# Rotation of 96 images by 180 degrees: the first load in three transfers instead of one

## The chip, the core and the metric

The kernel runs on one core of a Trainium2 chip. A core has several engines with instruction streams of their own, which meet at semaphores. Three matter here: VectorE (DVE in the profile) copies data within the on-chip memory; SyncE (SP) issues DMAs and waits for semaphores before it issues them; sixteen DMA engines move the data between HBM and the on-chip memory. The on-chip memory has 128 partitions, and a tile here is a row of float32 numbers in each of them.

The metric is the device time of one execution in microseconds (us), as the median of several runs.

## The reference

```
batch, c, h, w = 32, 3, 256, 256
x = np.random.randn(batch, c, h, w).astype(np.float32)

def reference(x):
    return np.rot90(x, k=2, axes=(-2, -1)).astype(np.float32)
```

Each of the 32 x 3 = 96 images of 256 x 256 is turned by 180 degrees. Read as a line of 65,536 numbers, an image is simply reversed. 25.17 MB are read and as many written.

## The kernel before

The 96 images are taken in three strips of 32 images. In a strip each image is cut into four quarters of `E` = 16384 numbers (64 KB), so that a strip fills 128 partitions with a row of 64 KB each, in tiles `A`, `Bt` and `Ct` for strips 0, 1 and 2. A fourth tile `T` of 2048 numbers per partition is scratch. All three strips lie on the chip at once; no tile is used twice.

The reversal is split in two. `inside` reverses each row in place on VectorE: for four pairs of blocks of 2048 numbers it copies the far block reversed into `T`, the near block reversed into the far place, and `T` into the near place (three copies a pair, all on line 52). The four quarters of an image change places in the store: the output is addressed with its quarters in reverse order (lines 58 and 59).

All DMAs are issued by SP, in the order of the code: the load of `A` (line 69), the load of `Bt`, then `Ct` in a body of 58 KB and a tail of 6 KB per row (`TAIL` = 1536 numbers), then the stores. They go through one queue, which its DMA engines empty in order. Strip `A` is stored in two pieces: the first 128 numbers of each row (`LEAD`), and the rest. The second of these also waits, by a dependency added by hand, until the body of `Ct` has landed. `Bt` and `Ct` are each stored in one piece when VectorE is done with them.

A copy on VectorE waits for the load of the numbers that it reads or overwrites, and a store for the copies that wrote its numbers. The framework places these waits: one semaphore for each DMA in flight, one for VectorE. Where an instruction has more waits than it can carry itself, the queue gets small waiting instructions ahead of it.

Of the kernel before, what the change touches and what calls it, by code (L numbers as in the profile page):

```python
# [2 lines left out]

os.environ.setdefault("NEURON_RT_ULTRASERVER_MODE", "4")

# [4 lines left out]


@with_exitstack
def kernel(
    ctx: ExitStack,
    tc: tile.TileContext,
    x: bass.AP,
    out: bass.AP,
):

    nc = tc.nc
    P = 128

    B, C, H, W = x.shape
    L = H * W
    G = 32
    E = L // 4
    J = E // 8

    x4 = x.rearrange("b c h w -> (b c) (h w)").rearrange(
        "(g n) (s e) -> g (n s) e", n=G, s=4)
    o4 = out.rearrange("b c h w -> (b c) (h w)").rearrange(
        "(g n) (s e) -> g n s e", n=G, s=4)  # L40

    pool = ctx.enter_context(tc.tile_pool(name="slots", bufs=1))
    A = pool.tile([P, E], x.dtype, tag="A")
    Bt = pool.tile([P, E], x.dtype, tag="B")
    Ct = pool.tile([P, E], x.dtype, tag="C")
    T = pool.tile([P, J], x.dtype, tag="T")

    def back(t, lo, hi):
        return t[:, hi - 1:(lo - 1 if lo else None):-1]

    def copy(dst, src):
        tc.keep_in_program_order(nc.vector.tensor_copy(out=dst, in_=src))  # L52

    def load(t, g, lo, hi):
        return nc.sync.dma_start(out=t[:, lo:hi], in_=x4[g][:, lo:hi])  # L55

    def store(t, g, lo, hi):
        return nc.sync.dma_start(
            out=o4[g][:, ::-1, lo:hi], in_=t[:, lo:hi])

    def inside(t):
        for lo in range(0, E // 2, J):
            hi = E - lo - J
            copy(T[:, :], back(t, hi, hi + J))
            copy(t[:, hi:hi + J], back(t, lo, lo + J))
            copy(t[:, lo:lo + J], T[:, :])

    TAIL = 1536
    load(A, 0, 0, E)
    load(Bt, 1, 0, E)  # L70
    body = load(Ct, 2, 0, E - TAIL)
    load(Ct, 2, E - TAIL, E)
    inside(A)
    LEAD = 128
    store(A, 0, 0, LEAD)
    first = store(A, 0, LEAD, E)
    tc.add_manual_dep(
        first.ins, body.ins.name,
        mybir.DependencyInfo(mybir.DependencyClass.Sync, mybir.DependencyReason.DATA),
        reason="the first store is queued while the last strip is on its way")  # L80
    for g, t in ((1, Bt), (2, Ct)):
        inside(t)
        store(t, g, 0, E)


# [1 line left out]
_INS = ['x']  # L87
_OUTS = [((32, 3, 256, 256), 'float32')]


# [23 lines left out]
```

## Time and profile before

| | us |
|---|---|
| median of 7 runs | 122.16 |
| lowest and highest run | 121.97, 122.73 |
| the profiled execution | 122.0 |
| its span in the profile | 120.2 |
| VectorE busy, 36 copies of 1.227 us | 44.2 |
| DMA: 50.33 MB in 1152 packets, 419 GB/s over the span | |

The profiled execution's time is 1.8 us longer than its span, which runs from the first instruction in the profile to the last. A packet is what one DMA engine moves as one piece: here one row of a transfer, or the 4-byte message to a semaphore that ends a transfer on that engine. A transfer of 128 rows gives each of the sixteen engines eight rows and one such message. The share of a DMA queue is the time that its packets took, as a part of sixteen engines' time in the stretch that is asked for. Rows of SP's queue have the start and the duration of the issuing instruction; the time to landing runs from the issue until the last message has come.

### The profile page before, as it was taken

How to read it: one execution, taken by the hardware profiler on the slowest of the kernel's cores; microseconds unless marked ns; L12 is line 12 of the kernel's file. 1: busy time of each engine (PE TensorE's matmuls, PEld its weight loads, DVE VectorE, ACT ScalarE, POOL GpSimd, SP SyncE). 2: the span in 40 equal slices, each digit the busy share in tenths (PEclk: the TensorE clock that was granted, in tenths of full speed). 3: DMA queues.
4: the chain of work that ended last, by engine and by line, in shares of the span. 5: the costliest groups of instructions: out<-in, count | busy, mean ns of one | idle time of the engine just before them, and what ended most of it. 6: DMA issues, size and time to landing. Idle time of an engine off the chain costs nothing.

```text
span 120.2 us, 95 instructions
## 1 busy us (share of the span) xinstructions
DVE 44.2 (37%) x36; POOL 0.2 (0%) x4
## 2 busy tenths in 40 slices
DVE  0000000499995099999059999400000000000000
POOL 0000000000000000000000000000000000000000
DMA  9888988899889979879499777988898889888980
GB/s 349 349 349 349 676 371 349 349 632 414 349 349 611 403 316 573 375 316 632 192 438 692 346 346 346 692 349 349 349 698 349 349 349 698 349 349 349 676 371 0
DMA packets 1152, 50.33 MB, mean 419 GB/s; under 512 B 128, under 2 KB 256, under 8 KB 384
## 3 DMA queue, kind: packets, MB, share of 16 engines
q1 hardware_dynamic: 1152, 50.33, 97.4%
HBM read 25.17 MB, written 25.17 MB: 419 GB/s over the span
## 4 chain that ended last, share of the span: by engine, by line
DMA 34%; DVE 25%; another core or an unknown queue 4%; issue 1%; SPq 0%; DVEq 0%
DMA Bt<-in_x_dram 34%; DVE T L52 8%; DVE Bt L52 8%; DVE Ct L52 8%; SPq L55 0%; DVEq L52 0%
## 5 line engine op out<-in xcount | busy, mean ns | idle before, releaser
L52 DVE COPY T<-A 128x2048 f32<-128x2048 f32 x4 | 4.9, 1227 | 22.8 <-DMA A<-in_x_dram 22.7
L52 DVE COPY T<-Ct 128x2048 f32<-128x2048 f32 x4 | 4.9, 1227 | 4.5 <-DMA Ct<-in_x_dram 4.4
L52 DVE COPY T<-Bt 128x2048 f32<-128x2048 f32 x4 | 4.9, 1227 | 4.4 <-DMA Bt<-in_x_dram 4.3
L52 DVE COPY Bt<-T 128x2048 f32<-128x2048 f32 x4 | 4.9, 1227 | 0.1
L52 DVE COPY Bt<-Bt 128x2048 f32<-128x2048 f32 x4 | 4.9, 1227 | 0.1
L52 DVE COPY A<-A 128x2048 f32<-128x2048 f32 x4 | 4.9, 1227 | 0.1
L52 DVE COPY Ct<-T 128x2048 f32<-128x2048 f32 x4 | 4.9, 1227 | 0.1
L52 DVE COPY A<-T 128x2048 f32<-128x2048 f32 x4 | 4.9, 1227 | 0.1
L52 DVE COPY Ct<-Ct 128x2048 f32<-128x2048 f32 x4 | 4.9, 1227 | 0.1
L98 POOL MEMSET const-bfloat16-1.0<- 128x1 bf16 x1 | 0.1, 101 | 0.0
L98 POOL MEMSET const-uint8-127<- 128x1 uint8 x1 | 0.1, 101 | 0.0
L98 POOL MEMSET const-float32-0.0<- 128x1 f32 x1 | 0.1, 98 | 0.2 <-issue 0.2
L98 POOL MEMSET const-float32-1.0<- 128x1 f32 x1 | 0.1, 98 | 0.0
## 6 DMA issues: line engine op xcount, KB each, us to landing
out_dram<-A SPq DMA_DIRECT2D x1, 8128.0 KB, 21.2
Ct<-in_x_dram SPq DMA_DIRECT2D x1, 7424.0 KB, 57.9
Ct<-in_x_dram SPq DMA_DIRECT2D x1, 768.0 KB, 59.3
out_dram<-A SPq DMA_DIRECT2D x1, 64.0 KB, 35.2
A<-in_x_dram SPq DMA_DIRECT2D x1, 21.9
Bt<-in_x_dram SPq DMA_DIRECT2D x1, 40.8
out_dram<-Bt SPq DMA_DIRECT2D x1, 39.8
out_dram<-Ct SPq DMA_DIRECT2D x1, 42.8
```

Of the source, the lines that this page charges most:

```text
L52: tc.keep_in_program_order(nc.vector.tensor_copy(out=dst, in_=src))
L98: nc = _bacc.Bacc("TRN2", target_bir_lowering=False, num_devices=1)
```

## The change

Line 69 is replaced by a loop of three loads into the same tile. They bring the first 512 numbers of each row (2 KB), the next 1024 (4 KB) and the remaining 14848 (58 KB). They are issued one after the other ahead of the load of `Bt`. Nothing else is edited: `inside(A)`, which begins by reading the last 2048 numbers of a row and then overwrites them with the first 2048, now has waits for three loads instead of one, and the second store of `A` has waits for all of them.

```
     TAIL = 1536
-    load(A, 0, 0, E)
+    for lo, hi in ((0, 512), (512, 1536), (1536, E)):
+        load(A, 0, lo, hi)
     load(Bt, 1, 0, E)
     body = load(Ct, 2, 0, E - TAIL)
     load(Ct, 2, E - TAIL, E)
```

On SP, `load` stands before as one instruction for 128 x 16384 numbers and after as three, for 128 x 512, 128 x 1024 and 128 x 14848. The order of the instructions on VectorE is the same, and no other queue has DMAs.

More of the change, by code (lines that the diff above doesn't have):

```diff
@@ L68 @@
     TAIL = 1536
-    load(A, 0, 0, E)
+    for lo, hi in ((0, 512), (512, 1536), (1536, E)):
+        load(A, 0, lo, hi)
     load(Bt, 1, 0, E)
```

## The prediction

> **What bounds the kernel now.** I read the page first, for the engine that has no idle time.
>
> ```profile
> span 120.2 us, 95 instructions
> DVE 44.2 (37%) x36; POOL 0.2 (0%) x4
> ...
> DMA packets 1152, 50.33 MB, mean 419 GB/s; under 512 B 128, under 2 KB 256, under 8 KB 384
> ## 3 DMA queue, kind: packets, MB, share of 16 engines
> q1 hardware_dynamic: 1152, 50.33, 97.4%
> ```
>
> VectorE is busy for 37% of the span; the sixteen DMA engines for 97.4% of it. All eight DMAs go through one queue: 8 x 128 rows of data and 8 x 16 tiny completion packets make the 1152. To see where the other 2.6% lie, I asked for the DMA packets of the stretch from 1.7 to 119.1 us alone:
>
> ```profile
> q1 hardware_dynamic: 1152, 50.33, 99.8%
> ```
>
> So from the first packet to the last the engines hardly pause, and the idle time is the 1.7 us before and the 1.1 us after. A change here can act in three ways only: more packet time, a different start, or a new pause. Next, the waits of VectorE and of SP's queue:
>
> ```profile
> DVE T L52 <- DMA A<-in_x_dram: 22.7, 1, 22.7
> DVE T L52 <- DMA Ct<-in_x_dram: 4.4, 1, 4.4
> DVE T L52 <- DMA Bt<-in_x_dram: 4.3, 1, 4.3
> ...
> SPq L58 <- DMA Ct<-in_x_dram: 33.1, 2, 32.5
> ```
>
> VectorE always waits for loads, never a load for VectorE: it has 4.3 us to spare after strip A and 4.4 us after B. The SP line is the wait of the second store of A for the body of C (32.5 us), which sets when the store is queued.
>
> Now the price of a packet. The share of the queue, times 16 engines, times the length of the stretch, over the packets, is the mean time of one packet. The stretches are, in order, 5.5 to 19 us (64 KB rows of A), 42.6 to 55.5 (58 KB rows of C), 59.2 to 60.5 (6 KB rows of C's tail) and 118 to 120.2 (completions alone):
>
> ```profile
> q1 hardware_dynamic: 80, 5.24, 89.6%
> ...
> q1 hardware_dynamic: 96, 5.70, 102.0%
> ...
> q1 hardware_dynamic: 86, 0.53, 98.6%
> ...
> q1 hardware_dynamic: 16, 0.00, 0.4%
> ```
>
> They give 0.896 x 16 x 13.5 / 80 = 2.419 us, 1.020 x 16 x 12.9 / 96 = 2.193 us, 0.986 x 16 x 1.3 / 86 = 0.238 us, and 0.004 x 16 x 2.2 / 16 = 9 ns. (A packet counts whole where it begins, so a stretch can pass 100%.)
>
> Last, the start: SP's issues, and the packets that begin in 0 to 4 us, then in 1.75 to 2, 2 to 2.3 and 2.3 to 3 us.
>
> ```profile
> 0.73 0.38 SPq L55 DMA_DIRECT2D A<-in_x_dram  x1
> 1.16 0.43 SPq L55 DMA_DIRECT2D Bt<-in_x_dram  x1
> 1.63 1.01 SPq L55 DMA_DIRECT2D Ct<-in_x_dram  x2
> ```
> ```profile
> q1 hardware_dynamic: 16, 1.05, 77.4%
> ...
> q1 hardware_dynamic: 11, 0.72, 893.8%
> ...
> q1 hardware_dynamic: 3, 0.20, 176.4%
> ...
> q1 hardware_dynamic: 2, 0.13, 47.3%
> ```
>
> The first packets begin at 1.76 us, which is 0.65 us after SP has finished its first issue (0.73 + 0.38 = 1.11), and the last of the sixteen engines begins at 2.69 us in the packet records. The first packet of an engine takes 0.774 x 16 x 4.0 / 16 = 3.10 us on the mean, where later ones of the same size take 2.42: a start-up excess of 0.68 us. In the records it runs from 0.20 us (the engine that began last) to 1.09 us.
>
> **The change, part by part.**
>
> Packets. Each engine has 8 rows of a load. Two more DMAs are 16 more data packets and 2 more completions per engine; the bytes stay. What a packet costs beyond its bytes: 64 KB and 58 KB rows differ by 6144 bytes and 2.419 - 2.193 = 0.226 us, and a 6 KB packet takes 0.238, so 12 ns by the views; the packet records, whose medians are 2418, 2192 and 234 ns, give 8 ns. I take 8, since the stretch at 59.2 us holds a few packets that waited for the store behind them, and keep 12. That is 16 x 8 + 2 x 9 = 0.146 us, with 12 ns 0.21 us. It lies on the path, since the engines have no idle time that could cover it: **+0.15 us**.
>
> SP's issues. Two more of 0.43 to 0.48 us each put B's issue from 1.16 to some 2.1 us and C's tail from 2.1 to 3.0 us. Their packets are not due before A is read (20 us), so this is hidden for B and C. For A itself it is not free: the second transfer's issue ends near 1.59 us, its packets can begin 0.65 us later, at 2.24, and the third's at about 2.7. The first transfer occupies an engine for 8 rows of 2 KB at (0.226 / 3 + 0.008) = 83 ns, 0.67 us, plus at least the 0.20 us of excess: from 1.76 to 2.63 at the earliest. 2.24 comes before that. If the engines get their descriptors in turn over 0.93 us (1.76 to 2.69) and one DMA's turn begins after the last one's, the last engine begins its first transfer at 2.69, has done it at 3.56, and gets the second at 3.62: a pause of 0.06 us. The second lasts 8 x 0.158 = 1.27 us, past the third's arrival. I take 0 and keep 0.06.
>
> The start-up excess. No row shows a 2 KB packet as the first one. The bounds are that the whole mean excess goes (-0.68 us), and that it comes back once at each of the two new hand-overs (+1.36). I take 0: the first request goes out 0.65 us after the same first issue, the first issue is the same instruction, and the hand-overs that the trace has, from A to B and from B to C, show no excess (2418 to 2422 ns per packet on both sides of the first in the records).
>
> Waits. VectorE's first copy of A waits for the third transfer, which carries elements 14336 to 16383; the second, which reads the first 2048, waits for the other two, long landed. A few waits of under 0.1 us, within its 4.3 us. On SP the first store of A waits for the first transfer and that copy, as before; the second, queued behind the body of C, waits for two transfers more. SP's last satisfied wait stood 47 ns before the issue (59.528 to 59.575 us in the trace's SP rows), so two waits behind the body's could put the issue 0.09 us later. Behind that store on SP stand the stores of B and C, neither due yet (B's is issued at 60.2 and its packets start after 80 us). The cover of the second store is C's tail and the 512-byte store, 8 x 0.234 + 8 x 0.027 = 2.1 us (packet records). It is just used up: when each packet is joined to the one whose end it follows, four engines show pauses of 19 to 82 ns near 60.75 us, the only ones in the trace, and they end 0.25 us before the last engine. So a further 0.09 us on them does not reach the end; if it reached the last engine too, +0.09.
>
> Sum: 0.146 + 0 + 0 + 0 = +0.15 us. The profiled execution took 122.0 us, of which 120.2 is span and 1.8 lies around it: 120.2 + 0.15 + 1.8 = 122.15. The median of the runs is 0.16 above the profiled one, so **122.31 us**, +0.1%, where 0.3% (0.37 us) is about what a measurement of this kernel can tell from no change.
>
> The hand-overs that the trace has cost nothing that can be seen: 99.8% from first packet to last, over seven of them. What remains open is whether 0.67 us of work is enough to have the next DMA queued. A rule speaks against the change: the Trainium skill, "DMA: Bandwidth & Descriptors", section "Rules for kernel authors", asks for 1 MiB or more in each DMA (the first two transfers here are 0.26 and 0.52 MB), and the section "Anatomy of one DMA" gives a lone DMA issued from GpSimd a fixed cost of about 2.0 us. By that, two more DMAs would be an estimated +4.0 us, 126.2.
>
> **The rivals.**
>
> Faster: the start-up excess depends on the length of the first packets. For it: it is 0.68 us per engine, the only idle DMA time before the end that isn't SP's issue, and it is not one constant latency, since the engine that began last paid 0.20 and others up to 1.09. Against it: nothing ties it to length. All of it gone gives 122.31 - 0.68 = 121.63. It decides from 0.52 us on (0.37 + 0.15).
>
> Slower: the 2 KB transfer does not bridge to the second, so the engines pause, or the excess is paid again at a hand-over. For it: the margin is only 0.4 us for the first engine and -0.06 for the last. Against it: the full hand-overs elsewhere, with descriptors long queued. Paid once it gives 122.31 + 0.68 = 122.99, at both hand-overs 123.67. It decides from 0.22 us on (0.37 - 0.15).
>
> No effect even of the packets: were their 8 ns overlapped at the start, 122.16. That is the same class as my forecast.
>
> **How the numbers follow.** Same within 0.3%: 0.50, as the priced terms, 0.15 to 0.21 + 0.06 + 0.09 = 0.36, stay inside it; its own range is 122.1 to 122.5. Faster 0.24, slower 0.26: two unknowns of about equal size on both sides, the known cost leaning to slower. For eight in ten the range runs from the faster rival in full, 121.6, to nearly one repeated excess, 122.9.
>
> **What would show it.** 1440 packets, 160 under 512 B and 672 under 8 KB. The wait for A's load near 22.8 us instead of 22.65, B's and C's landings later by the same 0.15. The share from first packet to last still 99.8%. The forecast is wrong if the wait for A's load ends before 22.3 or after 23.1, which would put the difference in the first 5 us, or if the landings agree and the second store of A starts late.

## The result and the profile after

The changed kernel takes 123.31 us as the median of 13 runs (122.04 to 124.02), the kernel before 122.13 us in 34 runs beside them. The ratio is 1.0082, with a 95% interval of 1.0063 to 1.0101: **slower by 0.8%**, some 1.0 us. (The ratio leaves out runs over 1.5% above the kernel's fastest one, which are its three slowest; the plain medians are 1.2 us apart.) The forecast was 122.31 and no change that can be told, with a range of 121.6 to 122.9. It was wrong.

The profiled execution of the changed kernel took 123.59 us, with a span of 121.8 against 120.2. From its page, the span and the DMA lines:

```profile
span 121.8 us, 99 instructions
...
DMA packets 1440, 50.33 MB, mean 413 GB/s; under 512 B 160, under 2 KB 288, under 8 KB 672
## 3 DMA queue, kind: packets, MB, share of 16 engines
q1 hardware_dynamic: 1440, 50.33, 96.4%
```

The packet counts are the ones forecast. VectorE's waits (total, times, longest, in us):

```profile
DVE T L52 <- DMA A<-in_x_dram: 23.9, 1, 23.9
DVE T L52 <- DMA Ct<-in_x_dram: 4.6, 1, 4.6
DVE T L52 <- DMA Bt<-in_x_dram: 4.3, 1, 4.3
```

The load of A ends 1.2 us later than before, not 0.15; the two other waits are nearly as before. So most of the loss exists at 24 us and is carried along. Where it comes from is seen in the DMA view of three stretches of the changed kernel: from the first packet to the last (1.7 to 120.7 us), 4.55 to 6.2 us, and 61.4 to 62.2 us.

```profile
q1 hardware_dynamic: 1440, 50.33, 98.7%
...
DMA packets 1, 0.06 MB, mean 36 GB/s; under 512 B 0, under 2 KB 0, under 8 KB 0
...
DMA packets 4, 0.02 MB, mean 31 GB/s; under 512 B 0, under 2 KB 0, under 8 KB 4
```

The first line says that there is now idle time between the first packet and the last (99.8% before). The second is its source. Fifteen engines go from their 4 KB rows to the long ones without a pause and begin their first 58 KB row between 4.07 and 4.51 us, as the packet records show; **one, done with its 4 KB rows at 4.29 us like the others, begins at 4.94 us, 0.65 us later, and needs 3.23 us for it instead of 2.19**. At 8.17 us it has done its first row when the others ended theirs at 6.26 to 6.70. The late one stays late, since each engine moves its own eight rows of every transfer. The landing records of the third transfer have fifteen messages between 22.36 and 22.75 us, and the sixteenth at 23.84; for the body of C it is 59.25 to 59.65, and 61.02.

The third line shows what the others do meanwhile. The second store of A is issued when the body of C has landed on all engines, at 61.11 us instead of 59.58, and its first packet begins at 62.31 us, 1.2 us after the start of the issue. In the 0.8 us of the view only four packets begin, all four 6 KB rows, which the late engine alone still has. Joined packet by packet, the other fifteen pause for 1.0 to 1.5 us there. The late engine has no such pause, and the last landing of all moves from 119.40 to 120.94 us.

The sum for the profiled executions: +1.21 us at the last landing of A's load (22.63 to 23.84), of which 0.15 is packets; +1.51 at the body of C, where the late engine's last row took 2.56 us instead of 2.19 while the others worked on small packets; +1.54 at the last landing. The late engine's landing of A is 1.28 us behind the mean of the other fifteen: nearly all of that is two terms of equal size: it begins its long rows 0.64 us after their mean start, and has 0.67 us more of the start-up excess in them (1.03 us, all in the first row, against 0.36).

### The profile page after: what moved, and what is told of

It is laid out like the page before. It is cut to its first block, busy times and chain, and to the rows that moved or that the text cites. A ratio compares the mean times of both kernels' runs of the same rounds, so it can differ in the third digit from the quotient of the medians.

```text
span 121.8 us, 99 instructions
## 1 busy us (share of the span) xinstructions
DVE 44.2 (36%) x36; POOL 0.2 (0%) x4
## 2 busy tenths in 40 slices
DMA packets 1440, 50.33 MB, mean 413 GB/s; under 512 B 160, under 2 KB 288, under 8 KB 672
## 3 DMA queue, kind: packets, MB, share of 16 engines
q1 hardware_dynamic: 1440, 50.33, 96.4%
## 4 chain that ended last, share of the span: by engine, by line
DMA 34%; DVE 24%; another core or an unknown queue 4%; SPq 1%; issue 1%; DVEq 0%
DMA Bt<-in_x_dram 34%; DVE T L52 8%; DVE Ct L52 8%; DVE Bt L52 8%; SPq L55 1%; DVEq L52 0%
## 5 line engine op out<-in xcount | busy, mean ns | idle before, releaser
L52 DVE COPY T<-A 128x2048 f32<-128x2048 f32 x4 | 4.9, 1226 | 24.0 <-DMA A<-in_x_dram 23.9
```

## The experiments

Each is compared with the kernel before on the same chip: e1 to e4 ran on one, e5 to e8 on a second, e9 to e12 on a third, e13 to e15 on a fourth. Edits are shown against the changed kernel (against the kernel before for e7, e8 and e11 to e13); where only lines with + are shown for the load of A, they stand in place of its loop or line. A hand-over is an engine's step from the rows of one transfer to those of the next. "Late" means that an engine begins its first long row of A clearly after the others, having stood still at the hand-over. The theories, named by letters, are set out in the expectations.

**e1: without the 4 KB transfer.**

```
-    for lo, hi in ((0, 512), (512, 1536), (1536, E)):
+    for lo, hi in ((0, 512), (512, E)):
```

> The changed kernel without the 4 KB transfer: 2 KB, then 62 KB of each row. Theory A (lagging engine): where the short first transfers hand over to long rows, one of the sixteen DMA engines begins late, and it is never overtaken, so its delay is the kernel's. One short hand-over, with only 0.67 us of work ahead of it, is enough: the last landing of the load of A is 0.5 us or more behind the second last, and the time is +0.4 to +1.2 us over the kernel before (122.5 to 123.4). Theory B (number of transfers): each extra transfer costs the same 0.5 us, so half of the change's +1.0, near 122.65, with landings spread evenly. Theory C (barrier): the loss is the pause of the other engines in front of the second store of A; it follows the lag, as in A.

122.09 us, ratio 0.9995 (0.9982 to 1.0008): no change. All long rows begin between 2.66 and 3.11 us. From 3.2 to 5 us, before the first of them can have ended, no packet begins:

```profile
DMA packets 0, 0.00 MB, mean 0 GB/s; under 512 B 0, under 2 KB 0, under 8 KB 0
```

So a 2 KB transfer ahead, with 0.67 us of work in it, bridges to the next one. That refutes theory A in the form stated, and theory B, by which each transfer costs the same.

**e2: the same 6 KB ahead, in one transfer.**

```
+    for lo, hi in ((0, 1536), (1536, E)):
```

> 6 KB, then 58 KB of each row: the same bytes ahead of the long rows as in the change, in one transfer instead of two. Theory A, if the late engine comes from a queue that ran dry: the first transfer lasts 8 x 0.234 = 1.9 us and the next is issued 0.43 us after it, so no lag, and +0.08 us for 8 packets and a message (122.2). Theory A, if the late engine comes from short packets as such (engines that start nearly together and then hinder each other in the long rows): lag and +0.4 to +1.2 us remain. Theory B: +0.5.

122.04 us, ratio 0.9992 (0.9982 to 1.0001). The long rows begin at 4.15 to 4.55 us, at the same time as the fifteen of the change, and none is late: from 4.6 to 6.2 us, where the change has its late start, no packet begins.

```profile
DMA packets 0, 0.00 MB, mean 0 GB/s; under 512 B 0, under 2 KB 0, under 8 KB 0
```

With the same bytes in front, two transfers instead of three remove the loss.

**e3: three transfers, all long.**

```
+    for lo, hi in ((0, 4096), (4096, 8192), (8192, E)):
```

> Three transfers as in the change, but of 16, 16 and 32 KB of each row. Theory A: the first packets are long, the start-up excess is paid inside them as before (mean first packet 0.68 us above the later ones of its size), no engine lags: +0.15 us, 122.3. Theory B (number of transfers): +1.0, as the change.

122.06 us, ratio 0.9998 (0.9983 to 1.0012). Three transfers as such cost nothing that can be told.

**e4: the change without the gate of the second store.**

```
-    first = store(A, 0, LEAD, E)
-    tc.add_manual_dep(first.ins, body.ins.name, ...)
+    store(A, 0, LEAD, E)
```

> The changed kernel without the dependency of the second store of A on the body of C, so that this store is queued at about 41 us and no engine has to pause for it. Theory A: the lagging engine has no pause of its own, so the other engines' 1.0 to 1.5 us of pause vanish from the packet records and the time stays at +1.0 (123.1), the others being done early. Theory C (barrier): the time falls back to that of the kernel before, 122.1 to 122.4.

124.34 us, ratio 1.0179 (1.0154 to 1.0204): slower still. The pause at the second store is gone from the packet records, and the time did not fall to 122.4 as theory C wanted it, that the pause is the loss. In this profile four engines are late, beginning at 5.07, 5.40, 5.47 and 5.99 us, after pauses of 0.8 to 1.9 us at the hand-over from the second to the third transfer. The stretch from 4.45 to 6.2 us of this kernel:

```profile
DMA packets 4, 0.24 MB, mean 136 GB/s; under 512 B 0, under 2 KB 0, under 8 KB 0
```

**e8: the kernel before without that gate**, the control for e4, by the same edit.

> The kernel before without the dependency of the second store of A on the body of C; the control of the changed kernel without it. If what that one lost beyond the changed kernel (1.0 us more) belongs to the missing dependency, this one is 0.5 to 1.0 us slower than the kernel before; if it was only a larger lag at the start of those executions, this one takes 122.1 to 122.4, as the lag of its engines is small.

123.11 us, ratio 1.0062 (1.0033 to 1.0091). The gate is itself worth some 0.8 us, which accounts for most of the 1.0 us that e4 lost beyond the change. With it, theory C would have given e4 122.4 + 0.8 = 123.2 us; it took 124.3, so the pause of the fifteen is not the loss. Without the gate the change costs 124.34 - 123.11 = 1.2 us (on two chips), about what it costs with it. The page's row for the tail of C in this kernel (KB, us to landing) has 60.5 where the kernel before has 59.3:

```profile
Ct<-in_x_dram SPq DMA_DIRECT2D x1, 768.0 KB, 60.5
```

After four runs the question was why only the change's series has late engines. New theories said what delivers a transfer to an engine, and when.

**e5: four transfers, three of them tiny**, so that every engine runs dry at each hand-over.

```
+    for lo, hi in ((0, 128), (128, 256), (256, 384), (384, E)):
```

> The first load as four transfers, of 0.5, 0.5, 0.5 and 62.5 KB of each row. The short ones last only 8 x 0.027 = 0.2 us on an engine, so every engine runs dry at each hand-over and the first packet of each transfer shows when that transfer reached the engine. Theory D1 (one transfer after the other): spreading a transfer over the engines takes a fixed 0.9 us or more, so the first packets of the four come at about 1.8, 2.7, 3.6 and 4.5 us or later, with a spread over the engines. Theory D2 (two at a time): the third comes only after the first has landed, the fourth after the second. Theory D3 (delivery is slow only beside full data traffic): the four come 0.47 us apart as they are issued, at 1.8, 2.2, 2.7 and 3.2 us. Time: by D1 and D2 +1 to +2.5 us, by D3 +0.5 to +0.9.

123.49 us, ratio 1.0097 (1.0059 to 1.0136). The first rows of the last transfer begin from 3.18 us on, as theory D3 has it, and one after the other 0.9 us each (D1) is refuted: the fourth is there where D1 wanted it at 4.5 or later. With so little traffic the long rows begin on time, the first 0.65 us after the end of SP's issue (2.53 us); D2 is not told apart here. The time is above D3's bound, and the reason is in the stretch from 3.16 to 3.85 us, and in VectorE's wait:

```profile
q1 hardware_dynamic: 43, 1.03, 457.6%
```
```profile
DVE T L52 <- DMA A<-in_x_dram: 23.6, 1, 23.6
```

4.576 x 16 x 0.69 is 50.5 us; 27 of the 43 packets are small ones of some 27 ns, and the sixteen long ones take (50.5 - 0.7) / 16 = 3.11 us each, where the later ones take 2.36. The start-up excess, 0.75 us on the mean, is paid in full by the first long rows, although the engines had been at work since 1.75 us. With long rows that begin at 3.18 to 3.80 us instead of 1.76 to 2.69, that makes up the loss without a late engine.

**e6: the short transfer second, after a long one.**

```
+    for lo, hi in ((0, 4096), (4096, 4608), (4608, E)):
```

> The first load as 16, 2 and 46 KB of each row, so that the short transfer comes after 5 us of other work. Theory D1: the third transfer has been delivered by 6 us and is due at about 8 us: no pause, no lagging engine, +0.15 us. Theory D2: the third is delivered only after the first has landed at about 7.9 us, and the 2 KB transfer covers 0.67 us of the delivery: a pause of 0.5 us or more on all engines, +0.6 us or more.

121.99 us, ratio 0.9985 (0.9970 to 0.9999). The third transfer's rows begin at 7.80 to 8.25 us, on each engine right after its last 2 KB row, and on three engines before the first one's last message comes at 7.96. The pause of 0.5 us or more on all engines, by which D2 was to be known, is not there; D2 is refuted.

**e7: the change's split, but on the load of B.**

```
-    load(Bt, 1, 0, E)
+    for lo, hi in ((0, 512), (512, 1536), (1536, E)):
+        load(Bt, 1, lo, hi)
```

(A comes in one transfer.)

> A comes in one transfer again; the load of B is split into 2, 4 and 58 KB of each row instead, which is the same number of transfers, packets and messages, but their turn comes at 22 us, when all have long been issued. If the loss of the change comes from the hand-overs of the first 5 us: no pause, no lagging engine, +0.15 us (122.3). If short transfers ahead of long ones cost this wherever they stand: +1.0.

122.09 us, ratio 0.9988 (0.9973 to 1.0002). The same packets and messages at 22 us cost at most what was priced. The loss belongs to the first microseconds. (The change itself was not run on the chip of e5 to e8, so that e6 and e7 have no late engine beside them there; e1 and e2 have one on theirs with e4, and e14 with e13 and e15.)

**e9: the changed kernel again.**

> The changed kernel once more, for a second profile. Theory D3 (the descriptors of the third transfer reach some engines late because the first two already move data at full rate): again one or more engines begin their 58 KB rows 0.4 us or more after the others, though not the same delay, since the runs of this kernel lie between 122.04 and 124.02; the last landing of A's load minus 22.63 us (the kernel before) gives the lag of the span within 0.4 us. If no engine is late and the span is over 121 us, the theory falls.

123.8 us, ratio 1.0134 (1.0116 to 1.0151). Four engines are late this time, at 5.15, 5.17, 5.85 and 6.13 us, twelve begin between 4.17 and 4.59. The stretch from 4.62 to 6.2 us, and VectorE's wait:

```profile
DMA packets 4, 0.24 MB, mean 150 GB/s; under 512 B 0, under 2 KB 0, under 8 KB 0
```
```profile
DVE T L52 <- DMA A<-in_x_dram: 24.5, 1, 24.5
```

The last landing of A's load is at 24.43 us, 1.80 later than before; the span is 122.0, 1.8 longer. Which engines are late, and by how much, differs from execution to execution. The ratio here, of three runs, lies above the first one's interval (1.0063 to 1.0101), so the price of the change is no fixed number: some 1.0 us there and 1.6 here.

**e10: each short transfer twice as long.**

```
+    for lo, hi in ((0, 1024), (1024, 3072), (3072, E)):
```

> 4, 8 and 52 KB: as many transfers and as many descriptors ahead of the long rows as in the change, each short one twice as long, so the long rows are due at about 1.76 + 0.4 + 8 x (0.159 + 0.31) = 5.9 us instead of 4.1 to 4.5. Theory D3 (late delivery, up to 4.9 us in the change's profile and 6.0 in that without the gate): most of the loss is gone, 0 to +0.4 us. Theory E (the engine stumbles after a given number of descriptors, 18, or at the second message, whenever that is): +1.0 us as the change.

122.4 us, ratio 1.0024 (1.0011 to 1.0037), so 0.3 us where the change itself lost 1.6 on the same chip (e9). The long rows begin at 6.11 to 6.86 us, none late, after as many packets and messages as in the change. Theory E is refuted. The 0.3 us that remain agree with the packets' 0.15 and a little more start-up excess (0.86 us per engine on the mean of the packet records, against 0.68 before), paid mostly by the 4 KB packets here (up to 1.41 us for one).

**e11 and e12: delivery measured by itself.** Five loads of 0.5 KB per row from ScalarE's queue, beside 16 KB rows from SP, and alone.

```
+    for n in range(5):
+        nc.scalar.dma_start(out=T[:, n * 128:(n + 1) * 128], in_=x4[1][:, n * 128:(n + 1) * 128])
```

(The edit is e11's, which also loads A in 16 and 48 KB per row; e12 has the five in A and ahead of SP's first load, which overwrites them, with SP's loads kept in the order of the code. One run each.)

> A comes as 16 and 48 KB from SP, and beside it ScalarE's queue issues five loads of 0.5 KB per row into the scratch tile (work that the change does not have), so that the time tells little; the start of the 512-byte packets tells when each of the five was delivered while 16 KB packets of 0.61 us keep the engines busy until about 7 us. Issued 0.47 us apart from 0.73 us, they are due at 1.8, 2.2, 2.7, 3.2 and 3.6 us. Theory D3: the later ones come 0.5 us or more beyond that plus a packet of 0.61 us, on some engines over 1 us beyond. If delivery is not slowed: all within 0.65 us of the due time.

> The same five loads of 0.5 KB per row from ScalarE's queue, but SP's first load waits for them, so that they are delivered with no other traffic (the whole kernel begins some 4 us later by that). Both theories: first packets within 0.2 us of 1.8, 2.2, 2.7, 3.2 and 3.6 us on all engines.

Alone (126.32 us in all), they came on time: the first packets of the five at 1.74, 2.28, 2.79, 3.27 and 3.71 us, the last of each at most 0.55 us after its first, where 0.2 had been expected on all engines. Beside traffic the measurement failed (and VectorE's first copy waited until 62.8 us for the five loads into `T`, so that the kernel took 140.35 us). The two queues took turns packet by packet, so a packet's start tells when its turn came, not when it was delivered: from 8 to 42 us each began 286 packets. From 0 to 8 us, with ScalarE's queue as q10:

```profile
q1 hardware_dynamic: 160, 2.88, 90.3%
q10 hardware_dynamic: 144, 0.07, 2.8%
...
T<-in_x_dram ACTq DMA_DIRECT2D x5, 64.0 KB, 41.0
```

**e13: e2 with a tiny transfer between the two**, which makes the long rows third.

```
+    load(A, 0, 0, 1536)
+    load(T, 1, 0, 128)
+    load(A, 0, 1536, E)
```

> 6 KB and 58 KB of A, as in the version of two transfers that cost nothing, but SP issues a load of 0.5 KB per row into the scratch tile between them (work that the change does not have; it lasts 0.22 us on an engine). The long rows are thus the third transfer, issued at 1.63 us, and due after 8 x 0.234 + 0.22 = 2.1 us of work, a little more than in the change, with no 2 KB packet and no split of the 6 KB. Theory D3 (position and issue time of the long rows): late engines as in the change, +0.5 to +1.5 us. Theory F (2 KB packets and their hand-over): no late engine, +0.1 to +0.3.

122.49 us, ratio 1.0038 (1.0018 to 1.0058), with runs from 122.28 to 123.47. The profiled execution is the slowest of ten runs, and in it one engine pauses for 1.28 us and begins its long rows at 5.71 us, the others at 4.29 to 4.97. From 5 to 6.5 us:

```profile
DMA packets 1, 0.06 MB, mean 40 GB/s; under 512 B 0, under 2 KB 0, under 8 KB 0
```

No 2 KB packet and no split of the 6 KB is needed for a late engine, and theory F, by which there was to be none, is refuted for this execution. The median is another matter: its 0.32 to 0.46 us (by medians and by the ratio) lies between F's range and D3's, and 0.22 us of it are the added transfer's own work. So most executions may have no late engine, or one that is hardly late. And here the long rows are third and also issued 0.46 us later than in e2; the run doesn't tell the two apart.

**e14: the change's three transfers, the last two exchanged.**

```
+    for lo, hi in ((0, 512), (1536, E), (512, 1536)):
```

> The three transfers of the change with the last two exchanged: 2, 58, 4 KB. Same packets, messages and issues; the long rows are issued second, at 1.16 us, and the third transfer is due only at 20 us. Theory D3: no late engine, as with 2 and 62 KB, 0 to +0.15 us. Theory B (number of transfers at the start, or more issues in a row on SP): +1.0.

122.06 us, ratio 0.9990 (0.9978 to 1.0003), no engine late: the long rows begin at 2.61 to 3.16 us, and from 3.2 to 5 us no packet begins, as in e1. This undoes the loss by the order alone.

**e15: four short transfers of 2 KB.**

```
+    for lo, hi in ((0, 512), (512, 1024), (1024, 1536), (1536, 2048), (2048, E)):
```

> 2, 2, 2, 2 and 56 KB of each row: four short transfers of 0.67 us each, issued 0.47 us apart, the long rows fifth, issued at 2.6 us and due after 2.7 us of work, near 5 us. Theory D3 (delivery under full traffic is late by up to 2 to 3 us on some engines): pauses of some engines already between the short transfers, from the third on, and long rows that begin late on several: +1 us or more. If only the third transfer is slow for some reason: pauses there alone, and the fifth on time.

123.73 us, ratio 1.0131 (1.0088 to 1.0175). The landings of the four spread out as they go on: 2.79 to 3.66 us, 3.72 to 4.28, 4.50 to 5.71, 5.33 to 6.94. Some engines pause already between the short transfers, from about 3.5 us on, and the long rows begin anywhere from 5.01 to 6.61 us. It isn't the third alone.

What the runs show together: the long rows begin on time when their transfer is the second (e1, e2, e14), when it is due only at 6 us or later (e3, e6, e10, and B in e7), and when there is little traffic (e5, e12). In a series of three or more with the engines at full rate and a turn that comes at 3.5 to 5 us, one or several engines go without their next rows, for 0.65 us in the change and up to 2.1 us in e9 (the others are e4, e13 and e15). **The latest engine then sets the time**: the waits for A's load of 22.5 to 22.7 us go with spans of 120.1 to 120.3 where the gate stands, 23.0 with 120.6, and 23.6 to 24.5 with 121.7 to 122.0 (e14 stands apart, since its first copy waits for the second of its three transfers alone). That delivery to an engine is what is late, and not the engine that fails to take it up, is the reading that these conditions suggest. No run separates the two, since the profile has no record of a delivery. Nor does any run tell whether what SP goes on to issue in those microseconds, the loads of B and C (until 3.51 us in the change), has a part in it. That a late engine makes the loss is shown; why it is late is open.

## Why the prediction was wrong, point by point

- **Packets, +0.15 us: right.** 1440, 160 and 672 were counted. In the change's profile the fifteen engines that were not late landed A at 22.36 to 22.75 us, the kernel before at 22.16 to 22.63.
- **SP's issues, taken as 0 with 0.06 kept: this step failed.** It let the third transfer reach every engine at about 2.7 us, 0.65 after the end of its issue, a distance read where nothing was moving yet, and so allowed for no pause behind 1.9 us of work. One engine paused for 0.65 us there and began the third only at 4.94 us (the change); in e9 it was 6.13 and in e4 5.99 on the latest. Whether the transfer came late to it or was taken up late stays open. The 0.06 was worked out for the second transfer, where nothing went wrong. The step's comparison also named the wrong hand-over as the narrow one: the 0.67 us of the 2 KB transfer suffice (e1, e14), while after the two together, 8 x 0.083 + 8 x 0.158 = 1.9 us of work, an engine stood still.
- **The start-up excess, taken as 0: nearly right in sum, wrong in place.** It does not vanish with short first packets. In the change's packet records it is 0.77 us per engine on the mean, against 0.68 before: 0.27 in the 2 KB rows, 0.09 in the 4 KB rows, and 0.40 in the long rows, of which the second to fourth take up to 2.50 us instead of 2.19. But the late engine has 1.03 us of it in its first long row, and that row is on the path. e5 shows it returning in full, 0.75 us, in the first long rows. The faster rival, that it depends on the length of the first packets, has next to nothing left: no version was faster by 0.3%.
- **The slower rival was the right one in kind**, an engine that pauses and pays again at a hand-over, and its price for one repeated excess, 122.99 us, was nearest to the result, though only just (it is 0.32 us off, 123.67 for two 0.36), and in part by luck: the loss of A's load is about half pause and half excess on one engine, not a mean excess paid once more by all. It put the pause on the first hand-over and on all engines; it fell on one to four engines at the second, and the worst engine counts, not the mean. Its chance, 0.26, was too low, because the evidence against it, hand-overs that cost nothing, came from transfers issued 20 us before their turn, and so says nothing about one issued 2.5 us before.
- **The extra waits of SP: right.** The issue came 0.08 us after the last landing of C's body, against 0.06 before.
- **The rule** of the Trainium skill, "DMA: Bandwidth & Descriptors", section "Rules for kernel authors", of 1 MiB or more per DMA spoke against the change and was right on the sign here. The 2.0 us that the page gives for a lone DMA issued from GpSimd, +4.0 us by the estimate, is not what happens on SP's queue, and small transfers as such cost nothing that can be told: e1, e2 and e14 put transfers of 0.26 to 0.79 MB first at no cost, and e7 two of them in the middle.
- **What would show it**: the wait for A's load ended at 23.9 us, after the 23.1 that had been named as the sign of an error in the first 5 us. That sign was right.

## What to carry to other kernels

Leave room between the issue of a transfer and its turn, and don't take the margin seen without traffic for the one beside it. Here the first packet came 0.65 us after the end of the issue with little traffic (e5), and up to some 4 us after it on single engines in a series of short transfers (2.07 to 6.13 us in e9). One transfer of 2 or 6 KB per row ahead of the long rows was free here (e1, e2); a second one was not where the long rows' turn came at 4 to 5 us, and cost 0.3 us where it came at 6 (e10). Where each DMA engine has its own rows, read the last of the sixteen landings and not the mean: one engine that landed A 1.1 us after the next cost the kernel that much to its end.

## What was not expected of the hardware

Two queues on the same DMA engines took turns by packet, and not by bytes, with the sizes used here (e11): 64 KB in rows of 0.5 KB beside rows of 16 to 64 KB took 41.0 us in the median to land, and 2.1 us alone (the same loads in e12). And to hold the store of A back until the body of C has landed is worth 0.8 us (e8), though the queue is emptied in order either way: without the gate the tail of C lands 1.2 us later after its issue. Why was not followed up.
